# A later gate for GpSimd's casting DMAs, and three stores cut in halves, in a fused two-matmul kernel

## Chip, cores and metric

One core of one Trainium2 chip. Times are device microseconds of one execution; each was timed several times, and medians with the lowest and highest are given. Differences of a few tenths of a microsecond are within the scatter of single executions.

## The reference

```python
# x (16, 512, 768), w1 (768, 3072), b1 (3072,), w2 (3072, 768), all float32
y = np.matmul(x, w1) + b1
y = 0.5 * y * (1.0 + erf(y / np.sqrt(2.0)))      # GELU
return np.matmul(y, w2).astype(np.float32)
```

## The kernel before

Both products are done with a Strassen-like scheme in float16. In the opening SyncE loads the first four row tiles of x (128 rows of 768 float32, 393 KB each) and the first block of W1 uncast; VectorE casts them. All else comes by casting DMAs, which GpSimd issues: W1 block 1, x tiles 4 to 7, W1 blocks 2 to 4, and so on. A one-column copy on GpSimd reads one of SyncE's x tiles, so that everything GpSimd issues waits for that tile. I call it the gate.

```python
for t in range(4):                                                   # SyncE: x tiles 0..3
    nc.sync.dma_start(out=xf[:, t, :], in_=xr[:, t, :])
for half in range(2):                                                # SyncE: W1 block 0
    r = slice(half * KQ, (half + 1) * KQ)
    nc.sync.dma_start(out=wf[:, r, :], in_=w1r[:, r, 0:2 * P])
# ... cut: bias, identity
nc.gpsimd.tensor_copy(out=xh_of(0, 4)[:, 0:1], in_=xf[:, 0, 0:1])    # the gate
load_wt(1)                                                           # GpSimd, casting: W1 block 1
for t in range(4, 8):
    load_x(0, t)                                                     # GpSimd, casting: x tiles 4..7
for n in range(2, 4):
    load_wt(n)
# ... cut: warm-up matmuls; casts and transposes of tiles 0..3; cast of W1 block 0
plain(0, 0, ...)      # first real matmuls: tiles 0..3 with W1 block 0
plain(1, 0, 0, 0)     # W1 block 1
transpose_pe(0, 4)    # tile 4, then plain, tile 5, plain, tile 6, ...
```

In the middle, quarters of W2 are stored to DRAM from SyncE, a few in each slot of TensorE's schedule; at the end the outputs are stored. SyncE's DMAs use eight completion semaphores ("lanes") in turn.

```python
def raw_w2(p):
    b11, _, b21, b22 = quarters(p)
    for n, b in ((1, b11), (2, b21), (3, b22)):
        raws.append(lambda p=p, n=n, b=b: nc.sync.dma_start(out=w2s[p, n][:], in_=b))
# ... cut; called in each slot of the unit:
drain(slot, 3 if U == 0 and slot > 1 else int(U + 1 == NU))
```

Of the kernel before, what the change touches and what calls it, by code (L numbers as in the profile page):

```python
# [22 lines left out]
def kernel(  # L23
# [8 lines left out]
    nc = tc.nc  # L32
# [10 lines left out]
    NU = RH // P  # L43
# [6 lines left out]
    NQ = NH // 2  # L50
# [8 lines left out]
    w2s = {(p, q): dp.tile([P, NQ, N4], F16, name=f"w2s{p}{q}")  # L59
           for p in range(1, 8) for q in range(1, 8)}  # L60
# [28 lines left out]
    def cut(off, n, pattern=None, **dims):  # L89
        ap = arena[:, off:off + n]  # L90
        return ap.rearrange(pattern, **dims) if pattern else ap
# [113 lines left out]
    with tc.manual_schedule():  # L205
# [9 lines left out]
        def sums(ns):  # L215

            for q in (soon, queue):
                while q and ns >= q[0][0] * 0.6:
                    ns -= q[0][0]
                    q.pop(0)[1]()  # L220

        def flush(q):
            while q:
                q.pop(0)[1]()
# [8 lines left out]
        def load_wt(n):  # L233
            hi = hi_of(n)
            if n >= NH:
                sb, k = divmod(n, NH)
                wts[n] = wt_far[k - 4] if 4 <= k < 7 else wt_late[(sb + 2 + k - 7 * (k > 6)) % 4]
                nc.sync.dma_start(out=wts[n], in_=w1s[hi][:])
                return
            wts[n] = slots[n]  # L240
            nc.gpsimd.dma_start(out=w1_raw(wts[n]), in_=w1r[:, :, 2 * hi * P:2 * (hi + 1) * P])
# [22 lines left out]
        puts, raws, LAG = [], [], [2]  # L264

        def quarters(p):
            w = w2v[SLOT[p]]
            return w[:, 0, 0:NQ, :], w[:, 1, 0:NQ, :], w[:, 0, NQ:NH, :], w[:, 1, NQ:NH, :]

        def split_w2(p, t, q=None, ns=(7, 5, 6, 4)):  # L270

            b11, b12, b21, b22 = quarters(p)

            def put(q, src, eng=nc.sync):
                eng.dma_start(out=w2s[p, q][:], in_=src)

            t = {n: spare[k] for n, k in zip((7, 5, 6, 4), t)}
            for n, a, b in ((7, b22, b12), (5, b12, b11), (6, b22, t[5]), (4, b21, t[6])):
                def f(n=n, a=a, b=b):
                    tt(t[n], a, b, SUB)  # L280
                    puts.append([LAG[0], lambda eng: put(n, t[n], eng)])
                if n in ns:
                    later(WB, f, slow if q is None else q)
# [5 lines left out]
        def raw_w2(p):  # L289
            b11, _, b21, b22 = quarters(p)  # L290
            for n, b in ((1, b11), (2, b21), (3, b22)):
                raws.append(lambda p=p, n=n, b=b: nc.sync.dma_start(out=w2s[p, n][:], in_=b))

        ORDER = (1, 6, 2, 7, 5, 4, 3)
        w2_order = [(ORDER[0], q) for q in (1, 2, 5, 6)]
# [16 lines left out]
        def xh_of(sb, t):  # L312
            if sb < ONE:
                return cut(sb * GR + GR // 2 + t * K, K)
            return xh_mid[t % 5 if t < 5 else t - 5] if sb == ONE else xh_late[t % 3]
# [33 lines left out]
        def g_sum(k, U, c0=0, c1=NH, q=None):  # L349
            G1, G2 = g_of(U // NU)  # L350
            r = slice(U % NU * P, (U % NU + 1) * P)
            g11, g21 = G1[:, c0:c1, 0, r], G1[:, c0:c1, 1, r]
            g12, g22 = G2[:, c0:c1, 0, r], G2[:, c0:c1, 1, r]
            s = [t[:, c0:c1, :] for t in GS]
            a, b, op = ((g21, g22, ADD), (s[0], g11, SUB), (g11, g21, SUB), (g12, s[1], SUB))[k]
            later((c1 - c0) * P, lambda: tt(s[k], a, b, op), q)
# [27 lines left out]
        def lev_sums(i, c0=0, c1=NQ, ks=(0, 1, 2, 3), q=None, m=None):  # L384

            A = OPERAND[ORDER[i]] if m is None else operand(*HYBRID[m])
            levs = None if m is None else hyb_lev[m]
            a11, a12 = A[:, c0:c1, 0:2 * P], A[:, NQ + c0:NQ + c1, 0:2 * P]
            a21, a22 = A[:, c0:c1, 2 * P:RH], A[:, NQ + c0:NQ + c1, 2 * P:RH]
            s = [t[:, c0:c1, :] for t in (lev_of(i) if levs is None else levs)]  # L390
            for k in ks:
                a, b, op = ((a21, a22, ADD), (s[0], a11, SUB), (a11, a21, SUB),
                            (a12, s[1], SUB))[k]
                later((c1 - c0) * 2 * P, lambda k=k, a=a, b=b, op=op: tt(s[k], a, b, op), q)
# [344 lines left out]
        xf = cut(GR, 8 * K).bitcast(FP32).rearrange("p (t k) -> p t k", t=4)  # L739
# [13 lines left out]
        nc.scalar.activation(out=zero[:, 1, 0:1], in_=zero[:, 0, 0:1], func=GELU)  # L753
        make_identity(nc, ident[:])
        make_identity(nc, idf)
        nc.gpsimd.tensor_copy(out=xh_of(0, 4)[:, 0:1], in_=xf[:, 0, 0:1])
        load_wt(1)
        for t in range(4, 8):
            load_x(0, t)
# [198 lines left out]
        def drain(slot, n=0, eng=nc.sync, wait=True):  # L958
            for f in puts:
                f[0] -= 1  # L960
            while puts and not (wait and puts[0][0] > 0):
                puts.pop(0)[1](eng)
            for f in raws[:n]:
                f()
            del raws[:n]

        def fill_mm2_one(sb, U, slot):
            if slot == 1:
                flush(queue)
                g_sum(2, U, q=soon)  # L970
                if U == 0:
                    g_sum(3, U, q=soon)
                flush(soon)
                if U == 0:
                    for p in (1, 2, 3, 5, 6, 7, 4):
                        raw_w2(p)
                    w4 = (6, 4, 5, 3)
                    split_w2(4, w4, ns=(5, 6, 4))
                    split_w2(1, (0, 1, 2, 6))
                    split_w2(2, (3, 0, 1, 2))  # L980
                    split_w2(4, w4, ns=(7,))
            drain(slot, 3 if U == 0 and slot > 1 else int(U + 1 == NU))
            if slot == 2:
                soon.extend(late)
                late.clear()
                if U + 1 < NU:
                    g_sum(0, U + 1, q=soon)
            if slot == 3 and U > 0:
                g_sum(3, U, q=soon)
            if slot == 4 and U + 1 < NU:  # L990
                g_sum(1, U + 1, q=soon)
            if U + 2 == NU and slot == 5:
                lev_sums(None, m=0, ks=(0, 1, 3))
            if U + 1 == NU and slot == 4:
                lev_sums(None, m=0, ks=(2,))
            if slot > 1:
                sums(1200)
            if slow and (U and slot > 1 or slot > 4):
                slow.pop(0)[1]()
                if slow and slot == 6:  # L1000
                    slow.pop(0)[1]()
            if slot == 6 and U + 1 == NU:
                flush(slow)
                flush(queue)
# [131 lines left out]
        for g, (kind, sb, k) in enumerate(units):  # L1136
            if g < 2:
                loads_a(g)
                if g:
                    transposes_a(g)  # L1140
                continue
            cur = kind(g, sb, k)
            if g < len(seq):
                period(cur, prev, lambda slot: fill_a(g, slot))
            else:
                f = {Unit1: fill_mm1, Unit2: fill_lean if sb else fill_mm2_one, UnitH: fill_hyb,
                     Unit3: fill_mm2_two}[kind]
                period(cur, prev, lambda slot: f(sb, k, slot))
            prev = cur
# [30 lines left out]
```

## Time and profile before

| | before |
|---|---|
| time, median of 6 (lowest to highest) | 851.34 us (851.04 to 851.8) |
| span of the profiled run | 848.7 us |
| TensorE busy | 843.3 us |
| x tile 3 / last W1 half of SyncE landed | 7.68 / 9.87 us |
| GpSimd's first issue / its first packet / W1 block 1 landed | 4.57 / 8.60 / 11.65 us |
| first real matmul / first matmul on W1 block 1 | 9.39 / 12.10 us |

TensorE is the bound: only what happens before its stream closes up, or after its last matmul, can move the time. Packet times and landings ("landed" is the last of a DMA's sixteen semaphore updates) are from the records of the trace.

### The profile page before, as it was taken

The numbers are of one execution on the slowest core, as the hardware profiler recorded it, in microseconds if no ns is written. First come the engines' busy times: TensorE is split into PE (matmuls) and PEld (weight loads), VectorE is DVE, ScalarE is ACT, GpSimd is POOL, SyncE is SP. The second block draws the span as 40 slices with busy tenths as digits, with TensorE's granted clock in tenths as the row PEclk, the third lists the DMA queues.
The fourth block names the chain that finished last, engine by engine and source line by source line (L and its number), as shares of the span: only waits on it lengthen the run. The fifth ranks groups of instructions, "written<-read, shape, count | busy, mean of one in ns | idle before, by whom it ended". The sixth has DMA issues, their size and how long they took to land.

```text
span 848.7 us, 16767 instructions
## 1 busy us (share of the span) xinstructions
PE 843.3 (99%) x6546; PEld 577.6 (68%) x6546; DVE 673.5 (79%) x1134; ACT 426.4 (50%) x700; POOL 94.9 (11%) x151
## 2 busy tenths in 40 slices
PE   9999999999999999999999999999999999999998
PEld 5444445796544897449964499545995469964798
DVE  5766679777857997679967799668996699957997
ACT  4777763231287413773247721587116761277611
POOL 5021100042200002000020000200002100010000
PEclk9999999999999999999999999999999999999999
DMA  9998796699998699987999489994999949984397
GB/s 228 216 274 166 166 221 232 233 201 221 361 329 206 207 341 370 255 201 259 335 368 300 118 296 346 359 276 123 319 356 335 281 114 324 369 300 168 106 308 282
DMA packets 144819, 222.11 MB, mean 262 GB/s; under 512 B 61964, under 2 KB 85444, under 8 KB 144740
## 3 DMA queue, kind: packets, MB, share of 16 engines
q1 hardware_dynamic: 117392, 178.85, 66.4%
q0 software_dynamic: 27168, 42.08, 22.4%
q8 instruction: 51, 0.84, 0.4%
q14 instruction: 28, 0.23, 0.1%
q10 hardware_dynamic: 180, 0.11, 0.0%
HBM read 181.78 MB, written 49.45 MB: 272 GB/s over the span
## 4 chain that ended last, share of the span: by engine, by line
PE 99%; DMA 1%; SPq 0%; DVE 0%; ACT 0%; issue 0%
PE bY L416 22%; PE bY L520 15%; PE bX L416 14%; PE bX L520 10%; PE bZ L416 7%; PE bW L416 7%; PE bZ L520 5%; PE bW L520 5%; PE bY L459 4%; PE bZ L459 2%; PE bW L459 2%; PE bY L608 2%; PE bX L608 1%; PE bX L459 1%; DMA arena<-in_x_dram 1%; PE bZ L608 1%
## 5 line engine op out<-in xcount | busy, mean ns | idle before, releaser
L210 DVE TENSOR_TENSOR arena<-arena 128x1536 f16<-128x1536 f16 (+6 forms) x638 | 409.8, 674 | 4.8 <-DMA arena<-arena 0.7
L416 PEld LDWEIGHTS <-arena 128*128 128x128 f16 x2016 | 196.6, 98 | 220.1 <-issue 0.5
L520 PEld LDWEIGHTS <-arena 128*128 128x128 f16 x3528 | 292.1, 98 | 8.2
L416 PE MATMUL bY<-arena 128*128 128x512 f16 (+1 forms) x864 | 214.5, 375 | 0.0
L639 DVE TENSOR_TENSOR arena<-bY,arena 128x512 f32<-128x512 f32 (+1 forms) x102 | 69.4, 680 | 118.2 <-PE bY L416 88.3
L632 ACT COPY bY<-bX 128x512 f32<-128x512 f32 (+1 forms) x145 | 79.6, 549 | 118.1 <-DVE arena L569 87.8
L520 PE MATMUL bY<-arena 128*128 128x192 f16 x1500 | 138.3, 246 | 0.0
L416 PE MATMUL bX<-arena 128*128 128x512 f16 (+1 forms) x576 | 138.3, 375 | 0.0
L432 ACT ACTIVATE arena<-arena,b1t 128x1024 f16<-128x1024 f32 x94 | 108.0, 1149 | 51.6 <-DVE arena L667 51.6
L652 ACT COPY arena<-bW 128x512 f32<-128x512 f32 (+1 forms) x149 | 81.9, 550 | 93.1 <-PE bW L520 43.9
L520 PE MATMUL bX<-arena 128*128 128x192 f16 x1020 | 93.1, 246 | 0.0
L667 DVE TENSOR_TENSOR arena<-bZ,arena 128x512 f32<-128x512 f32 (+1 forms) x102 | 69.2, 679 | 22.3 <-PE bZ L416 19.1
L416 PE MATMUL bZ<-arena 128*128 128x512 f16 (+1 forms) x288 | 76.2, 375 | 0.0
L416 PE MATMUL bW<-arena 128*128 128x512 f16 (+1 forms) x288 | 76.2, 375 | 0.0
L552 POOL DMA_DIRECT2D out_dram<-arena x42 | 30.5, 728 | 403.1 <-DVE arena L663 367.5
L683 ACT COPY bZ<-bY 128x512 f32<-128x512 f32 (+1 forms) x60 | 31.8, 529 | 80.8 <-PE bY L459 30.0
L437 ACT ACTIVATE arena<-bX,b1t 128x512 f16<-128x512 f32 x94 | 64.0, 681 | 9.8 <-PE bX L416 9.7
L437 ACT ACTIVATE arena<-bY,b1t 128x512 f16<-128x512 f32 x94 | 63.3, 674 | 0.0
L459 PEld LDWEIGHTS <-arena 128*128 128x128 f16 x432 | 42.2, 98 | 28.0 <-issue 0.2
L319 POOL DMA_DIRECT2D arena<-in_x_dram x60 | 33.7, 635 | 161.7 <-DMA arena<-arena 153.4
L520 PE MATMUL bZ<-arena 128*128 128x192 f16 x504 | 48.4, 246 | 0.0
L520 PE MATMUL bW<-arena 128*128 128x192 f16 x504 | 48.4, 246 | 0.0
(63 smaller groups left out, 426.8 us busy)
## 6 DMA issues: line engine op xcount, KB each, us to landing
arena<-w2s SPq DMA_DIRECT2D x299, 288.0 KB, 4.8
arena<-w1s SPq DMA_DIRECT2D x72, 672.0 KB, 7.0
out_dram<-arena POOLq DMA_DIRECT2D x46, 384.0 KB, 7.1
w2s<-arena SPq DMA_DIRECT2D x49, 288.0 KB, 4.5
arena<-in_x_dram POOLq DMA_DIRECT2D x60, 192.0 KB, 7.6
w1s<-arena SPq DMA_DIRECT2D x12, 672.0 KB, 5.9
arena<-in_w_dram POOLq DMA_DIRECT2D x17, 384.0 KB, 8.6
out_dram<-arena SPq DMA_DIRECT2D x13, 384.0 KB, 2.5
```

The lines of the kernel that those rows point to most:

```text
L210: nc.vector.tensor_tensor(out=o, in0=a, in1=b, op=op)
L319: nc.gpsimd.dma_start(out=xhs[t], in_=xr[:, sb * 8 + t, :])
L416: nc.tensor.matmul(out=dst[:, r:r + w], lhsT=w1_op(self.wt, slot)[:, c, :], rhs=a[:, c, r:r + w], start=first and c == 0 and r == 0, stop= ...
L432: nc.scalar.activation(out=self.G[1][:, hi, :, :], in_=self.tmp, func=GELU, bias=b1t[:, 2 * hi + 1:2 * hi + 2])
L437: nc.scalar.activation(out=self.G[0][:, hi, row, :], in_=bank[:, 0:RH], func=GELU, bias=b1t[:, 2 * hi:2 * hi + 1])
L459: nc.tensor.matmul(out=dst[:, 0:N2], lhsT=a, rhs=w[:, :, c, :], start=first and c == 0, stop=c == self.C - 1, skip_group_check=True)
L520: nc.tensor.matmul(out=dst[:, t * N4:(t + 1) * N4], lhsT=a, rhs=w[:, c, :], start=first and c == 0 and t == ts[0], stop=c == NQ - 1, skip_ ...
L608: nc.tensor.matmul(out=dst[:, t * N4:(t + 1) * N4], lhsT=a, rhs=self.w[q][:, c, :], start=first and c == 0 and t == 0, stop=c == NQ - 1, s ...
L632: nc.scalar.copy(out=bY[u.g % 2][:, 0:u.F], in_=bX[u.g % 2][:, 0:u.F])
L639: nc.vector.tensor_tensor(out=u.c22(), in0=bY[u.g % 2][:, 0:u.F], in1=w[:, 0:u.F], op=ADD)
L652: nc.scalar.copy(out=w[:, 0:u.F], in_=bW[:, 0:u.F])
L667: nc.vector.tensor_tensor(out=u.c12(), in0=bZ[:, 0:u.F], in1=w[:, 0:u.F], op=ADD)
```

## The change

GpSimd's first DMA is to keep out of the way of SyncE's loads until x tile 3 is there; and the three stores of one W2 product are cut in two, so that three more DMAs turn the lanes on and the last stores fall on the last lanes, for which SyncE waits last.

```diff
-                raws.append(lambda p=p, n=n, b=b: nc.sync.dma_start(out=w2s[p, n][:], in_=b))
+                for c in (slice(0, NQ // 2), slice(NQ // 2, NQ)) if p == 4 else (slice(0, NQ),):
+                    raws.append(lambda p=p, n=n, b=b, c=c: nc.sync.dma_start(out=w2s[p, n][:, c, :],
+                                                                             in_=b[:, c, :]))
@@
-        nc.gpsimd.tensor_copy(out=xh_of(0, 4)[:, 0:1], in_=xf[:, 0, 0:1])
+        nc.gpsimd.tensor_copy(out=xh_of(0, 4)[:, 0:1], in_=xf[:, 3, 0:1])
@@
-            drain(slot, 3 if U == 0 and slot > 1 else int(U + 1 == NU))
+            drain(slot, 3 if U == 0 and slot > 1 else 2 * int(U + 1 == NU))
```

## The prediction

> **What bounds the kernel now.** I read the page first, then the table by stage for the first 15 us, the chain that ended last for the first 20 us, the waits of each engine, and last the records of the final 4 us.
>
> ```profile
> PE 843.3 (99%) x6546; PEld 577.6 (68%) x6546; DVE 673.5 (79%) x1134; ACT 426.4 (50%) x700; POOL 94.9 (11%) x151
> PE 99%; DMA 1%; SPq 0%; DVE 0%; ACT 0%; issue 0%
> PE bX L766 <- DVE arena L752: 1.2, 1, 1.2
> PE bT L333 <- DVE arena L772: 0.2, 1, 0.2
> ```
>
> TensorE is busy 843.3 of 848.7 us, 99% of the chain is TensorE, and of all its waits that have a named releaser 1.2 + 0.2 us are left. The remaining 848.7 - 843.3 = 5.4 us is split between the opening and the end. So no change of DMA issue can win more than some microseconds (0.6%), and it can win only before TensorE enters its gapless stream or after its last matmul. The opening, by stages of one microsecond (columns: TensorE, weight load, VectorE, ScalarE, GpSimd busy, clock, DMA share, GB/s):
>
> ```profile
> 3.00:4.00 1.00, 1.00 (x4) 0.32 (x3) 0.00 (x0) 0.00 (x0) 0.00 (x0) 1.00 1.03 409
> 4.00:5.00 1.00, 1.00 (x3) 0.26 (x2) 0.58 (x2) 0.00 (x0) 0.94 (x2) 1.00 1.05 356
> 5.00:6.00 1.00, 1.00 (x10) 0.74 (x9) 0.90 (x1) 0.32 (x1) 1.00 (x2) 1.00 1.02 264
> 6.00:7.00 1.00, 1.00 (x10) 0.50 (x8) 0.33 (x1) 0.84 (x3) 1.00 (x3) 1.00 0.98 363
> ```
>
> The DMA engines are full, at 409 GB/s, until GpSimd begins to issue at 4.57 us; then the rate sinks to 264 and comes back to 363. TensorE looks busy here, but these are warm-up matmuls and transposes; its useful stream begins at 9.39:
>
> ```profile
> 2.14 5.54 DMA arena<-in_x_dram
> ...
> 7.70 0.57 DVE arena L772
> 8.27 0.05 issue
> 8.32 0.52 PE bT L333 x6
> 8.84 0.02 issue
> 8.87 0.49 ACT arena L329
> 9.35 0.04 issue
> 9.39 0.81 PE bX L788 x3
> ```
>
> This chain (start, us, what) is the fourth x row tile landing at 7.68, its cast, its transposes, its copy, the first real matmul. From there the chain is TensorE without a hole. Who holds it close after that is seen in the waits of the weight loads that start a transpose, and in GpSimd's issues:
>
> ```profile
> 4.57 0.97 POOL L241 DMA_DIRECT2D arena<-in_w_dram  x1
> 13.62 0.43 PEld L333 LDWEIGHTS <-arena 128*128 128x128 f16 x6 [0.22 <-DMA arena<-in_x_dram]
> 14.57 0.46 PEld L333 LDWEIGHTS <-arena 128*128 128x128 f16 x6 [0.20 <-DMA arena<-in_x_dram]
> ```
>
> Tiles 5 and 6 of x come by GpSimd's casting DMAs and land at 13.57 and 14.53 by the semaphore records; their weight loads start 0.05 us later, and their transposes run at 13.73 and 14.71, where TensorE would have come to them anyway. Two chains arrive together: the loads on the SyncE queue that give the first matmuls, and the casting stream (W1 block 1, then x tiles 4 to 7) that feeds what follows.
>
> **What the Trainium skill says.** "DMA: Bandwidth & Descriptors", section "SWDGE vs HWDGE vs iDMA": a DMA that casts has to come from GpSimd, which writes its descriptors into rings in SBUF from where the DMA engines fetch them. That gives a possible cause for the dip to 264 GB/s; the trace shows the coincidence, not the cause. The same page, section "Queues, rings and completion order", says that each DMA engine takes turns between queues, packet by packet. The trace does not agree here: GpSimd's first DMA, issued at 4.57, has its first packet at 8.60, when the SyncE queue is nearly empty (its last packet ends at 9.56). Issues into a quieter queue had it after 1.44 to 1.58 us (issues at 77.54, 86.18, 101.50); the page's table "Specifications" gives about 1 us. So the early issue buys little: the bytes queue behind SyncE's anyway. "SBUF — State Buffer", section "Who interferes with whom", says that a VectorE cast in a two-port mode and GpSimd lock each other out. The trace fits: the cast of x tile 1, at 4.98 beside GpSimd's issue, took 0.92 us, the other three 0.56.
>
> **The change, part by part.** *Part A, the gate.* GpSimd's one-column cast, after which all its DMAs stand, waits for x tile 3 instead of tile 0. No engine's compute order changes; only its waits. Landings now, from the semaphore records: x tiles 4.00, 4.96, 6.64, 7.68; W1 halves 8.79, 9.87. The first step of 0.96 us is 393 KB at 409 GB/s. If the dip comes from GpSimd's descriptors, tiles 2 and 3 follow at that pace: 5.92 and 6.88, so tile 3 is 0.8 us early, and the W1 halves come at about 7.95 and 9.0 to 9.4 (GpSimd starts inside the second). The first matmul then stands at 6.88 + (9.39 - 7.68) = 8.6 instead of 9.39.
>
> But GpSimd starts later. Before: landing 4.00, cast at 4.06, issue at 4.57. After: landing 6.88, issue at 6.88 + 0.57 = 7.45, first packet 1.44 to 1.58 us later, at 8.9 to 9.0, perhaps 9.2. The casting stream now: 160 GB/s of written bytes in 9.0 to 9.5 and about 200 after, with a trickle from 8.60, which is as if it had started at full rate at 9.0. So the stream starts 0.1 us early to 0.2 late, I take 0.1 late. It then runs at the same 205 GB/s (0.95 us per x tile), so W1 block 1 lands near 11.65 + 0.1, tiles 5 and 6 near 13.67 and 14.63. TensorE can use them about 0.1 us after landing, and now passes them with some 0.05 us to spare. TensorE reaches W1 block 1 at 11.3 to 11.6 instead of 12.10, waits there, and goes on at the old pace: of the 0.5 to 0.8 us won at the front nearly all is given back, and after tile 6 the end has moved by about 0.1 - 0.05 = +0.05 us. The later blocks have room: W1 block 2 lands at 17.46 and is used at 20.94.
>
> *Part B, the halves.* Three stores of W2 quarters (295 KB each, contiguous) become six, two per slot in place of one. SyncE pays three issues of about 0.43 us more (their spacing at 158 us), 1.3 us, in a stretch where its queue is idle for microseconds at a time (from 151 to 156, and 165 to 175), with no TensorE wait there. Every later SyncE DMA moves by three of eight completion semaphores ("lanes"); the DMA eight before is still the one waited for, so the steady state is unchanged. At the end SyncE waits for the lanes in order. Before, the last stores sit on lanes 1 to 4: the wait for lane 3 (the last to land, 847.59) ends at 847.61, then four waits with nothing left to wait for start at 847.67, 847.73, 847.79 and 847.85. After, the last two stores sit on lanes 6 and 7, and one such wait follows: three times 0.06 = 0.18 us less.
>
> The sum: 851.17 + 0.05 - 0.18 = 851.04. A change of this care was probably kept because it won a little, and GpSimd's start may come out on the better side of my band: I lower it by 0.1 and say 850.95 us.
>
> **Rivals.** (1) *The dip is not GpSimd's.* Against GpSimd as cause: the rate recovers to 363 by 6 to 7 us while it still issues x tiles, and three W1 issues from 7.86 to 10.35 do not show such a dip. Then tile 3 still lands at 7.68, GpSimd issues at 8.25, the first packet comes at about 9.75, and everything after W1 block 1 moves 0.7 us back: +0.7 - 0.05 - 0.18, about 851.6. I give it one in four. (2) *The gate gains fully.* Packets start as soon as SyncE's queue is empty, at 8.6, and tiles 5 and 6 land 0.3 to 0.4 us early; TensorE gains as much: 851.17 - 0.35 - 0.18 = 850.6. For it: SyncE's queue really ends earlier if the dip goes. Against: 1.44 us from issue to first packet is the least seen. (3) *The shifted lanes or more store DMAs make a new wait* in the middle. Against: TensorE has no DMA wait there, and SyncE's slack is microseconds; at most some tenths.
>
> **Range and chances.** The rivals span 850.6 to 851.6; runs of before spread by 0.5 us. I take 850.1 to 851.9. A move of 2% would be 17 us, and all idle of TensorE is 5.4 us, so faster by 2% is impossible but for an accident, and slower would need a new stall of a kind that no step here has.
>
> **What would show it.** In the changed kernel: between 4 and 6 us the DMA rate stays near 400 GB/s and tile 3's cast starts near 6.9 (step 1; rival 1 if 7.7). GpSimd's first issue at 7.45, first packet near 9.0. The first real matmul near 8.6, and then a new TensorE wait of some tenths before the matmuls on W1 block 1, near 11.7 (the give-back). The weight loads for tiles 5 and 6 near 13.7 and 14.7 again; if they stand at 13.3 and 14.3, rival 2 holds. From 30 to 840 us the chain runs with the same durations, shifted by a constant. At the end one empty wait, not four, between the last landing and the final barrier. The prediction is wrong if the shift after 20 us is over 0.4 us either way, or if a TensorE wait on a DMA appears after 150 us.

## The result, and the profile after

The changed kernel takes 852.73 us (median of 6, 852.54 to 853.31) against 851.34: 1.39 us more, outside the predicted 850.1 to 851.9. The ratio is 1.0018 (95% interval 1.0005 to 1.003): small, but clear of noise. Such a ratio, here and below, is the mean time of one kernel's runs over that of the other's of the same rounds, so not quite the ratio of the medians. The span of the profiled run is 850.7 us, 2.0 more; the profile of before caught one of its better runs (a second one, below, had 849.0).

The page's busy line and chain, after:

```profile
PE 843.5 (99%) x6546; PEld 577.2 (68%) x6546; DVE 673.2 (79%) x1134; ACT 426.7 (50%) x700; POOL 95.0 (11%) x151
PE 98%; DMA 1%; POOL 0%; SPq 0%; DVE 0%; issue 0%
```

TensorE does the same work in the same time (843.5 against 843.3), so the 2.0 us are idle time. Its waits (who waited for whom: us in total, times, longest) name it; they sum to 3.4 us, against 1.4 in the two lines of before that the prediction shows:

```profile
PE bX L768 <- DVE arena L754: 1.2, 1, 1.2
PE bX L790 <- DMA arena<-in_w_dram: 1.0, 1, 1.0
PE bT L335 <- DMA arena<-in_x_dram: 0.6, 2, 0.3
PE bT L335 <- DVE arena L774: 0.4, 2, 0.2
PE bX L790 <- DVE arena L782: 0.2, 1, 0.2
```

The second and third line are new and the largest change: W1 block 1, then x tiles, each landing late. (Line numbers are two higher than before.) The stages that the prediction showed, after, with the same columns:

```profile
3.00:4.00 1.00, 1.00 (x4) 0.33 (x3) 0.00 (x0) 0.00 (x0) 0.00 (x0) 1.00 0.96 366
4.00:5.00 1.00, 1.00 (x8) 0.45 (x7) 0.56 (x1) 0.00 (x0) 0.00 (x0) 1.00 1.03 375
5.00:6.00 1.00, 1.00 (x12) 0.62 (x10) 0.56 (x1) 0.71 (x2) 0.00 (x0) 1.00 1.01 344
6.00:7.00 1.00, 0.76 (x9) 0.27 (x7) 0.56 (x1) 0.84 (x3) 0.00 (x0) 1.00 0.99 367
```

GpSimd is silent in all four, and the rate does not stay at 409 either. Tile 3 lands at 7.44, 0.24 us earlier instead of 0.8. Then the stages after SyncE's loads, which decide, first of the kernel before, then of the changed one:

```profile
8.00:9.00 1.00, 0.91 (x10) 0.45 (x8) 0.45 (x2) 0.76 (x2) 1.00 (x2) 1.00 1.08 345
9.00:10.00 1.00, 0.86 (x5) 0.38 (x4) 0.88 (x3) 0.72 (x2) 1.00 (x2) 1.00 1.42 210
10.00:11.00 1.00, 1.00 (x5) 0.31 (x4) 0.96 (x2) 0.00 (x0) 0.35 (x1) 1.00 1.45 202
...
13.00:14.00 1.00, 1.00 (x13) 0.64 (x11) 0.00 (x0) 0.72 (x2) 0.57 (x2) 1.00 1.15 206
```

```profile
8.00:9.00 1.00, 0.92 (x8) 0.45 (x8) 0.42 (x2) 0.68 (x2) 1.00 (x3) 1.00 0.73 256
9.00:10.00 1.00, 0.76 (x5) 0.39 (x5) 0.91 (x3) 0.49 (x2) 1.00 (x2) 1.00 0.17 16
10.00:11.00 1.00, 1.00 (x7) 0.41 (x6) 0.90 (x3) 0.00 (x0) 1.00 (x3) 1.00 1.02 124
11.00:12.00 1.00, 1.00 (x5) 0.29 (x3) 0.36 (x1) 0.52 (x1) 1.00 (x2) 1.00 1.43 193
12.00:13.00 1.00, 0.02 (x1) 0.00 (x0) 0.00 (x0) 0.75 (x2) 1.00 (x3) 1.00 1.31 209
13.00:14.00 1.00, 0.82 (x3) 0.21 (x3) 0.91 (x3) 0.00 (x0) 1.00 (x3) 1.00 1.09 137
```

(About 205 GB/s is full rate here: a casting DMA is counted by the half-size bytes that it writes.) Before, the casting stream takes over from SyncE's loads without a hole. After, three things are lost: the engines stand empty from 9.2 to 9.7 us (16 GB/s), the stream starts slowly (124), and it stumbles again at 13 us (137). The timeline shows the same from the engines' side (start and length in us, engine, line, operation; in brackets how long the engine stood idle before it, and what ended that; PEld and LDWEIGHTS are TensorE's weight loads):

```profile
7.49 0.57 POOL L758 CAST arena<-arena 128x1 f16<-128x1 f32 x1 [5.68 <-DMA arena<-in_x_dram]
8.00 0.97 POOL L241 DMA_DIRECT2D arena<-in_w_dram  x1
...
13.04 0.33 PEld L790 LDWEIGHTS <-arena 128*128 128x128 f16 x3 [1.52 <-DMA arena<-in_w_dram]
...
15.60 0.34 PEld L335 LDWEIGHTS <-arena 128*128 128x128 f16 x6 [0.74 <-DMA arena<-in_x_dram]
...
16.58 0.34 PEld L335 LDWEIGHTS <-arena 128*128 128x128 f16 x6 [0.32 <-DMA arena<-in_x_dram]
```

Put against the same instruction of the kernel before, TensorE's shift is -0.14 us at the first real matmul, +0.95 at W1 block 1, +1.47 at tile 4, +1.87 at tile 5, +2.14 after 45 us, and +2.17 at the last matmul. The step of +0.26 comes around 44 us, where VectorE waits for a DMA transpose of the next x tiles and TensorE for VectorE. It is not the late gate's alone: in the other profiles but e6 the same step is -0.11 to +0.45, and +0.45 is e2's, with the old gate. At the end 0.18 us come back: from the last landing to the end of the program is 1.15 us before and 0.97 after.

### The profile page after: what moved, and what is told of

It reads as the page before. It is cut to its first block, busy times and chain, and to the rows that moved or that the text cites. A ratio compares the mean times of both kernels' runs of the same rounds, so it can differ in the third digit from the quotient of the medians.

```text
span 850.7 us, 16771 instructions
## 1 busy us (share of the span) xinstructions
PE 843.5 (99%) x6546; PEld 577.2 (68%) x6546; DVE 673.2 (79%) x1134; ACT 426.7 (50%) x700; POOL 95.0 (11%) x151
## 4 chain that ended last, share of the span: by engine, by line
PE 98%; DMA 1%; POOL 0%; SPq 0%; DVE 0%; issue 0%
PE bY L418 22%; PE bY L522 15%; PE bX L418 14%; PE bX L522 10%; PE bZ L418 7%; PE bW L418 7%; PE bZ L522 5%; PE bW L522 5%; PE bY L461 4%; PE bW L461 2%; PE bZ L461 2%; PE bY L610 2%; DMA arena<-in_x_dram 1%; PE bX L610 1%; PE bX L461 1%; PE bZ L610 1%
```

## The experiments

Gate n alone means the kernel before with its gate on tile n. "Lead" is the time from GpSimd's first issue (in e5 the first after the gate) to the end of SyncE's last data packet of the opening. "Late packets" are those of GpSimd's queue that took over 250 ns, up to 20 us (a normal one takes 60 or 135). Each row is from one profile; times are medians, each against the kernel before.

| run | gate, extra | lead | first packet after issue | W1 block 1 after SyncE's last landing | late packets | time minus before |
|---|---|---|---|---|---|---|
| before | 0 | 4.94 | 4.03 | 1.77 | 0 | |
| e14 | 0, again | 5.25 | 3.77 | 1.65 | 4 | -0.2 |
| e2 | 0, halves | 6.20 | 4.12 | 1.65 | 0 | -0.1 |
| e3 | 1 | 5.18 | 3.08 | 1.83 | 0 | +0.1 |
| e4 | 2 | 2.13 | 1.68 | 2.80 | 12 | +1.0 |
| after | 3, halves | 1.17 | 1.68 | 3.40 | 24 | +1.4 |
| e10 | 3, halves, again | 1.12 | 1.67 | 3.57 | 23 | +1.7 |
| e1 | 3 | 1.06 | 1.68 | 3.38 | 22 | +2.5 |
| e11 | 3, again | 1.04 | 1.66 | 3.46 | 26 | +2.3 |
| e5 | 3, warm-up DMA | 1.07 | 1.53 | 3.40 | 19 | +2.4 |
| e6 | 3, hold | 1.12 | 1.67 | 3.27 | 21, then 8 | +5.0 |
| e8 | 3, filler 393 KB | 2.14 | 1.81 | 3.66 | 26 | +3.3 |
| e9 | 0, filler 393 KB | 5.55 | 4.53 | 1.71 | 0 | +0.7 |
| e12 | 3, filler 1180 KB | 4.08 | 2.99 | 1.92 | 1 | +4.3 |
| e13 | 0, filler 1180 KB | 9.29 | 4.49 | 0.95 | 0 | +3.9 |
| e7 | none | 10.93 | 4.06 | before it | 0 | +2.6 |

**The change in its two parts, and the gate in steps.** e1 is the gate alone, e2 the halves alone, e3 and e4 the gate on the tiles between.

```diff
-        nc.gpsimd.tensor_copy(out=xh_of(0, 4)[:, 0:1], in_=xf[:, 0, 0:1])
+        nc.gpsimd.tensor_copy(out=xh_of(0, 4)[:, 0:1], in_=xf[:, 3, 0:1])   # e1; e3: 1, e4: 2
```

> The gate of the change alone, without the halved stores. Theory (late stream): the whole loss is GpSimd's late first issue, whose bytes then arrive after the DMA engines have run dry. Expected +1.5 us over the kernel before (the changed kernel's +1.4 plus the 0.18 that the halves save at the end), the first matmul on W1 block 1 again near 13.0 us, TensorE 2.1 us late after 45 us. Rival (the shifted completion lanes or the extra stores cost something in the middle): this run is within 0.2 us of the kernel before.

> The halved stores alone, with the old gate. Theory: 0.18 us less than the kernel before, with no TensorE wait between 150 and 200 us, and after the last landing one empty lane wait instead of four. Rival (lanes): 0.5 us or more over the kernel before, with a new wait in the middle.

> The old stores, the gate on x row tile 1 (lands at 4.96 us). Theory (late stream): GpSimd's first issue moves from 4.57 to about 5.55, its first packet can come from 7.1 on, but SyncE's queue is only empty near 9 us, so the casting stream starts and ends as before: time within 0.2 us of the kernel before. Rival (each microsecond of gate delay costs[...]): +0.4 us or more. Second rival (GpSimd's issue beside SyncE's loads slows them): 0.2 to 0.4 us faster.

> The old stores, the gate on x row tile 2 (lands at 6.3 to 6.6 us). Theory (late stream): issue at about 6.9 to 7.2, first packet possible at 8.5 to 8.8, just as SyncE's queue runs empty: time 0 to 0.3 us over the kernel before, clearly under the gate on tile 3. If instead the slow ramp of the stream after a late start (71 GB/s in the half microsecond after 10.0) costs by itself and not the gap, this run shows the ramp too and is 0.5 us or more slower.

Measured: e1 853.89 us against 851.34 (ratio 1.0032, 1.0019 to 1.0044); e2 851.2 (0.9998, 0.9986 to 1.0011); e3 851.43 (1.0002, 0.9989 to 1.0014); e4 852.34 (1.002, 1.0006 to 1.0034). So the loss is the gate's, and it begins between tile 1 and tile 2. The halves cost nothing in the middle. Their 0.18 us is too small for these times, but the traces have it exactly: from the last landing to the end it is 0.97 us in all three kernels with the halves, and 1.15 to 1.16 in nine profiles with the old lanes. The four runs with a filler, whose one more DMA turns the lanes by one, have 1.09 to 1.10: 0.06 us for each lane turned.

e4 missed its expectation of 0 to 0.3 us. There the first packet came at 8.93 us, before SyncE's last at 9.38: no dry gap at all, and the stream still started slowly. That was the case named beforehand for the slow start costing by itself. e1 missed too, by 1 us upward.

**Is it a cold queue, or a dry one?** e5 sends a small casting DMA through GpSimd's queue ahead of the gate; e7 has no gate; e8 and e9 put a load that nothing reads behind SyncE's W1 halves, with the late gate and with the old one.

```diff
+        nc.gpsimd.dma_start(out=cut(GR + 8 * K + 8 * KQ * P + 4 * P, 64), in_=xr[:, 4, 0:64])  # e5, before gate 3
-        nc.gpsimd.tensor_copy(out=xh_of(0, 4)[:, 0:1], in_=xf[:, 0, 0:1])                      # e7
+        nc.sync.dma_start(out=cut(GR + 8 * K + 8 * KQ * P + 4 * P, 2 * K).bitcast(FP32),       # e8 (gate 3),
+                          in_=xr[:, 4, :])                                                     # e9 (gate 0)
```

> Gate on x row tile 3, and before the gate one small casting DMA from GpSimd (64 columns of an x tile to an unused place, 16 KB written), so that GpSimd's queue has run once before its first large load. Rival (cold queue): the slow first microsecond of the casting stream (71 GB/s, then 178) goes away, W1 block 1 lands 0.5 us or more earlier after GpSimd's issue than the 5.0 and 4.85 us of the two kernels with that gate, and the run is about 1.8 us over the kernel before instead of 2.5. Theory (late stream, dry engines): the ramp stays, the run stays near +2.5 us.

> No gate at all: GpSimd issues W1 block 1 from about 1.8 us on, beside SyncE's own issues (0.74 to 3.6). If bytes issued earlier to SyncE's queue really go first, as the kernels with gates on tiles 0 and 1 look, W1 block 1 is ahead of only a part of SyncE's loads here, and x row tiles 2 and 3 and W1 block 0 land later by the casting bytes that slip between: the first real matmul 1 to 3 us later, W1 block 1 no later than before; time +0.5 to +1.5 us over the kernel before. If the queues are strictly first come, first served: within 0.3 us.

> Gate on x row tile 3, and one more load of 393 KB on SyncE's queue behind the W1 halves, which nothing reads. Theory (late stream, dry engines): the filler occupies the engines for the 0.96 us in which they ran dry, and GpSimd's descriptors wait ready behind it, so the stream starts at full rate: no slower than the gate on tile 3 without it (+2.5), rather some tenths faster, and equal within 0.4 us to the next run, which has the old gate and the same filler. Rival (what costs is GpSimd's late issue by itself, wherever the bytes of SyncE end): filler and gate add up, +3 us or more.

> The old gate (tile 0) and the same filler. Theory: 393 KB more at 409 GB/s ahead of the casting stream, so the stream and with it the end move by 0.96 us: +0.7 to +1.1 us over the kernel before. If the opening is not bound by the bytes ahead of the casting stream, under +0.3.

Measured, against 851.27: e5 853.7 (1.0025, 1.0013 to 1.0037), e7 853.84 (1.0034, 1.0022 to 1.0046), e8 854.56 (1.0035, 1.0023 to 1.0047), e9 851.99 (1.0009, 0.9996 to 1.0022). The warm-up DMA changed nothing: W1 block 1 still lands 4.8 us after its issue. e9 did what more bytes should.

e8 was the test of my theory that the *dry engines* cost. In e8 the engines never run dry (GpSimd's first packet 10.10, SyncE's last 10.43), yet the stream starts slowly and stumbles as before:

```profile
10.00:11.00 1.00, 1.00 (x6) 0.48 (x5) 0.93 (x3) 0.00 (x0) 1.00 (x2) 1.00 0.75 109
11.00:12.00 1.00, 1.00 (x7) 0.39 (x4) 0.68 (x2) 0.24 (x1) 1.00 (x3) 1.00 1.39 186
12.00:13.00 1.00, 0.31 (x2) 0.00 (x0) 0.00 (x0) 1.00 (x2) 1.00 (x2) 1.00 1.37 198
13.00:14.00 1.00, 0.00 (x0) 0.00 (x0) 0.00 (x0) 0.03 (x1) 1.00 (x2) 1.00 1.22 147
14.00:15.00 1.00, 0.43 (x2) 0.16 (x3) 0.42 (x2) 0.00 (x0) 0.39 (x2) 0.69 0.86 140
15.00:16.00 1.00, 1.00 (x5) 0.40 (x4) 0.66 (x2) 0.00 (x0) 0.60 (x2) 0.50 1.17 195
```

W1 block 1 lands 3.66 us after SyncE's last load, as with the late gate alone, where the theory had the stream start at full rate; so the theory fell. e8's time says less. The last two rows show why: after 2.3 us without a matmul TensorE lost its clock (0.69, then 0.50; it stood at half for 3.41 us). Tile 6 landed at 17.38 us and TensorE came to it at 18.76, while in the changed kernel it came 0.05 us after the landing (16.54 and 16.59). So by my estimate about 1.3 us of the profiled run are the clock's. The two of e8's five runs that kept it (mean clock 0.999 and 1) took 853.31 and 854.01 us, 2.0 and 2.7 over the kernel before: about what the gate alone costs, and more than e9. That filler and late gate add up, as the rival had it, is not shown.

e7 shows why there is a gate at all. Without it W1 block 1 lands at 11.65, as early as before, but its bytes slip between SyncE's, whose last W1 half lands at 13.12 instead of 9.87, so that TensorE's second group of matmuls comes 2.97 us late. The loss was larger than expected.

**Is the stumble GpSimd's own later issues? Do the halves gain a microsecond?** e6 holds W1 blocks 2 to 4 back until x tile 7 has landed; e10 and e11 are the changed kernel and the gate alone once more, side by side.

```diff
+        nc.gpsimd.tensor_copy(out=xh_of(1, 0)[:, 0:1], in_=xhs[7][:, 0:1])    # e6, with gate 3
         for n in range(2, 4):
             load_wt(n)
```

> Gate on x row tile 3, and GpSimd issues W1 blocks 2 to 4 only when x row tile 7 has landed, so that nothing is issued while tiles 4 to 7 flow. Theory (a casting DMA whose packets follow at once on its issue is slow, and issues beside a running stream disturb it): the second stumble goes; tiles 4 to 7 land 0.95 to 1.0 us apart, no packet over 250 ns in the 2 us after W1 block 1 has landed. Then the next three blocks start from a dry queue, so a new gap of some 1.7 us plus a slow start follows tile 7, and the whole run is no faster: 1.5 to 3.5 us over the kernel with the gate alone. Rival (the stumble belongs to these bytes of x or to their place in memory): tile 5 or 4 lands 1.4 us or more after its predecessor again.

> The changed kernel once more, beside the gate alone on the same chip. The first comparison had it 1.16 us faster than the gate alone, in other calls and on another chip, where 0.18 was expected of the halves. Expected here: 0.1 to 0.4 us faster than the gate alone, and 1.4 to 2.5 us over the kernel before. Rival (the halves gain more than the end of the chain shows): again 1 us or more faster.

> The gate alone once more: 1.6 to 2.7 us over the kernel before, casting stream with a first packet 1.7 us after GpSimd's issue, some 20 packets over 250 ns in it before 20 us, and none in the kernel with the old gate.

Measured, against 851.19: e6 856.17 (1.006, 1.0047 to 1.0074), e10 852.86 (1.0019, 1.0006 to 1.0031), e11 853.44 (1.0026, 1.0014 to 1.0039). In e6 GpSimd issues nothing from 11.6 to 17.6 us, and tile 5 still lands 1.58 us after tile 4, with ten packets taking over 250 ns between 13.3 and 13.7; the wait before its transpose is there as in the changed kernel:

```profile
15.71 0.34 PEld L333 LDWEIGHTS <-arena 128*128 128x128 f16 x6 [0.84 <-DMA arena<-in_x_dram]
```

So the stumble is not made by later issues: that idea fell as well. e6 also shows the slow start a second time in one run: its held-back issue at 17.73 us, into a queue that had been empty since about 17.3, has its first packet at 19.28 and eight late packets by 19.84 (the table counts them apart).

e10 was 0.58 us faster than e11, where 0.18 is the halves' and the single times overlap (852.48 to 853.56, and 853.12 to 854.3). The rest, and most of the 1.16 us between the first calls, I take for scatter of the opening: at 45 us TensorE is 2.14 and 3.19 us late in the two profiles with the halves, 3.11 and 2.63 without. More runs would have to show it.

**Lead.** The table then suggested one quantity: long leads go with a clean start, short ones with a slow one. But until now lead had gone together with the gate: every late gate had a short one. e12 and e13 part them by a filler of three x tiles; the late gate now has a lead of 4 us. e14 is a second profile of the kernel before.

```diff
+        nc.sync.dma_start(out=cut(o_x1 + XT_N, 6 * K).bitcast(FP32).rearrange("p (t k) -> p t k", t=3),
+                          in_=xr[:, 4:7, :])                        # e12: gate 3; e13: gate 0
```

> Gate on x row tile 3, and a filler of 1180 KB (three x tiles, 2.9 us at 409 GB/s) behind the W1 halves on SyncE's queue, so that SyncE's bytes end about 4 us after GpSimd's first issue instead of 1.1 (gate alone) or 2.1 us (small filler). Theory (lead): what counts is how long before its packets can flow a casting DMA is issued; with a lead of 4 us the stream starts at full rate with at most a few packets over 250 ns, W1 block 1 lands 1.6 to 2.1 us after SyncE's last load, and the run equals the next one (old gate, same filler) within 0.5 us. Rival (lateness in itself, or the place of those bytes): W1 block 1 again 3.4 us or more after SyncE's last load, packets over 250 ns as in the gate alone, and 1.5 us or more over the next run.

> The old gate (tile 0) with the same filler of 1180 KB. Expected from the small filler (393 KB gave +0.7 us): about three times that, +2.2 to +3 us over the kernel before, with a casting stream that starts at full rate.

> The kernel before once more, for its profile: no packet over 250 ns in the casting stream before 20 us, W1 block 1 landing 1.6 to 1.9 us after SyncE's last load, and the landing of x row tile 3 somewhere from 7.4 to 8.8 us, as the runs with the old gate and those with the late gate both scatter.

Measured, against 851.28: e12 855.62 (1.0052, 1.0039 to 1.0064), e13 855.14 (1.0048, 1.0034 to 1.0062), e14 851.1. The two kernels with the filler differ by 0.48 us in their medians, where gates 3 and 0 without it differ by 2.3 to 2.5. The clock is in it again: e12's profile loses it (0.50 from 16.48 us, for 3.41), e13's does not. Of the runs that kept it (mean 0.999 or 1), e12's one took 854.05 us and e13's three 854.18 to 855.14. In the two profiles W1 block 1 landed at 15.16 and 15.15 us, tile 6 at 18.03 and 18.01: the late gate costs these landings nothing. In e12 W1 block 1 lands 1.92 us after SyncE's last load, as in the kernels with the old gate, with one late packet; the stream takes over at once and does not stumble:

```profile
11.00:12.00 1.00, 1.00 (x7) 0.47 (x5) 0.93 (x3) 0.00 (x0) 1.00 (x3) 1.00 1.05 379
12.00:13.00 1.00, 0.73 (x4) 0.11 (x2) 0.10 (x1) 0.81 (x2) 1.00 (x3) 1.00 1.35 224
13.00:14.00 1.00, 0.00 (x0) 0.00 (x0) 0.00 (x0) 0.45 (x1) 1.00 (x2) 1.00 1.44 200
14.00:15.00 1.00, 0.00 (x0) 0.00 (x0) 0.00 (x0) 0.00 (x0) 0.58 (x1) 1.00 1.24 209
15.00:16.00 1.00, 0.79 (x3) 0.21 (x3) 0.75 (x3) 0.00 (x0) 0.56 (x1) 1.00 1.16 207
```

The gate, the order and the bytes of GpSimd are those of e1; only SyncE's queue is longer. That decides for lead against lateness in itself, on one profile of each and on their times. e13 rose more than forecast (+3.9 against 2.2 to 3); its profile has an unrelated wait of 0.9 us for W1 near 690 us. The old gate starts clean only nearly always: e14 has four late packets, against its expectation of none; e2 and the first profile have none.

One rival has no run of its own: the interference between VectorE's casts and GpSimd that the prediction names. For the stumble e8's trace speaks against it: VectorE does nothing from 11.71 to 14.55 us, and thirteen packets that start from 13.19 to 13.76 are late. For the slow start it stays open, for in every run with gate 2 or 3 VectorE casts W1 block 0 beside GpSimd's issues (8.60 to 10.18 us in the changed kernel); in e12 it does so too, and with the long lead it does no harm.

No version beats the kernel before clearly. The best is e2, the old gate with the halves: 851.2 against 851.34 us, inside the scatter, with 0.18 us shown at the end of its trace.

## Why the prediction was wrong

- **The bound: right.** TensorE's busy time did not change, and everything happened in the first 45 us and the last 2.
- **Step 1, "the dip comes from GpSimd's descriptors": wrong.** From 4.5 to 6 us SyncE's queue moved 268 to 362 GB/s (mean 305) in the six profiles with gates 0 and 1, and 250 to 356 (mean 313) in the eight with gates 2 and 3 and no earlier GpSimd DMA, where GpSimd had issued nothing by then. Tile 3 landed at 7.42 to 8.79 us (mean 8.1) and 7.44 to 8.65 (mean 7.9). A gain of 0.8 us was counted where at most some tenths are, and scatter of over a microsecond hides them. What makes the dip stays open; it is in every profile. This is rival 1's premise, to which I gave one in four.
- **The stream's start, "0.1 us early to 0.2 late": wrong, the failing term of the sum.** I put it 0.1 us late, and W1 block 1 landed 1.35 us late (13.00 against 11.65). Of the difference, 0.58 us are the first packet at 9.68 instead of 9.1: the issue came at 8.00 instead of 7.45, as tile 3 was not early. The rest is a term that the sum did not have. From its first packet W1 block 1 needed 3.32 us, against 2.65 from the effective start at 9.0 before: 0.67 us of slow start. Then tile 5 came another 0.63 us late (+1.98) by the stumble. Rival 1 had the gap and allowed 0.7 us for it, but took the stream's rate for granted, so it fell short too.
- **What that term is.** GpSimd's early issue in the kernel before is not idle waiting behind SyncE's bytes, as the prediction had it ("the early issue buys little"). In these profiles a casting stream issued with a lead of 4 us or more takes over from SyncE's loads at full rate; with a lead of 1 to 2 us it starts slowly, with 12 to 26 late packets, and mostly stumbles about 3.4 us after its first packet. e12 against e1 and e13 shows that the lead decides. Why it does is not shown. The kernel before had the sign of it: its casting load issued at 101.50 us into an empty queue moved 73, 73 and 138 GB/s in its first three half microseconds, with 29 late packets. I had read only the 1.58 us to its first packet.
- **A misread line under "the early issue buys little".** The prediction took the first packet at 8.60, 4.03 us after the issue, as a disagreement with turn-taking between queues. Once both queues have packets, the traces do show turns: in e13, 45 to 48 of GpSimd's packets and 47 of SyncE's in each half microsecond from 10.5 to 12.5; in e7, 82 and 82 from 7.5 to 8.0. What holds the first packet back is not shown.
- **The give-back: right in kind.** TensorE did wait at W1 block 1, for 1.02 us, but there was next to no front gain to give back (0.14 us), so the lateness of the stream passed through: +1.87 at tile 5. I also took the later loads to have room. One transpose of the next x tiles, at the stream's end, had none, which made +2.14; but that step of 0.26 us is within what other profiles show without the late gate.
- **Part B: right.** -0.18 us at the end, no new wait in the middle. At the end SyncE's wait for the last landing is followed by one empty wait instead of four. (The prediction's first idle stretch of SyncE is 152.1 to 155.7 us in the trace, not 151 to 156; nothing hangs on it.)

## What to carry to other kernels

When an engine's DMA seems to be issued too early because its bytes move only later, look at the rate of its first microseconds before delaying it: the time in the queue may be doing work. Compare with a DMA of the same kind elsewhere in the trace that was issued into an empty queue; its start is what a delayed issue will look like. And where a dip stands beside an event in one profile, look for the dip in a run without the event before building a gain on it.

## What the Trainium skill lacked or had wrong

- "DMA: Bandwidth & Descriptors", section "Queues, rings and completion order", has the DMA engines take turns between queues packet by packet. The traces agree (e13, above: with packets of 512 and 3072 bytes that makes 46 to 49 GB/s for GpSimd and 289 for SyncE). What the page lacks is that the turns may begin late: in the profiles with gates 0 and 1, and in e7 and e12, GpSimd's first packet came 3.0 to 4.5 us after the issue, while SyncE's queue was full.
- The same page, "Specifications", gives about 1 us to the first byte of a GpSimd DMA. These runs have 1.42 to 1.81 us from the start of the issue to the first packet where GpSimd's queue was empty and SyncE's opening loads were over or had less than 0.5 us to go.
- No page has that the lead of a casting DMA decides its first microseconds: 1.65 to 1.92 us from SyncE's last landing to W1 block 1's in six profiles with leads of 4.1 to 6.2 us, 2.80 to 3.66 in eight with leads of 1.0 to 2.1.
- "TensorE: Matmul & The Clock Gate", section "What's actually happening", gives an idle window of about 3.4 us for the fall to half clock. Here gaps of 2.3 us (e8) and 2.5 us (e12) without a matmul were followed by 3.41 us at 0.50 each, while a gap of 2.8 us in e13's profile was not. Why is not shown.
